# An S5 stage with its y stores on other queues: burst outputs count as done one slot sooner, half of the stores of y on ScalarE, y's load and GELU issued sooner

## The chip, the core and the metric

The kernel runs on one core of a Trainium2 chip. It is timed in microseconds of device time, as the median of several runs. The core has engines that each run their own instructions in order: TensorE (PE, matrix products; its weight loads are shown apart as PEld), VectorE (DVE), ScalarE (ACT), GpSimd (POOL) and SyncE (SP). DMAs are begun by an instruction on one of the engines, mostly SP and POOL here, and then run beside them.

## What is computed

One step of a two-layer decoder trunk for 256 new prompt tokens and 8 sample tokens, 264 columns in all, in float32. The first layer is a short gated convolution, the second an S5 state-space mixer with a GLU. What matters here is the S5 mixer:

```python
proj = h @ w_in                       # 2048 -> 2 * 4096
u, z = jnp.split(proj, 2, axis=-1)
bu = einsum('tbgh,gph->tbgp', u, b_bar)
bu[0] += lam_bar * carry
states = associative_scan(a2*a1, a2*b1 + b2)      # over tokens, complex
y = real(einsum('ghp,tbgp->tbgh', c_c, states))
y = gelu(y + d_skip * u)
y = y * sigmoid(y @ w_glu + b_glu)                # 4096 -> 4096
out = (y * silu(z)) @ w_out                       # 4096 -> 2048
return out, real(h_last), imag(h_last)
```

There are 256 groups of 16 channels and 64 complex states.

## The kernel before

**Slots.** All weight products are cut into 640 slots, one for a block of 1024 x 128 weights: 24 matmuls of 264 columns, three for each of eight 128 x 128 blocks, since a float32 product is made of three products of split operands (wh times H, wh times L, wl times H). `load_raw` brings 1 MB of raw weights for two slots on SP (L187), `conv_h` makes wh on ACT (L196), `conv_l` makes wl on DVE (L205). Buffers: three of raw, four of wh, three of wl. Slots 320 to 383 make u, 384 to 447 make z, 448 to 575 the GLU (the first 18 of them, 448 to 465, need y tiles 0 to 23; slot 466 and on needs y tiles 24 to 31), 576 to 639 the output.

**The order.** `Stream.go` writes the program out slot by slot: per slot the raw load six slots ahead, then the running procedures (generators), then wh three slots ahead, wl two ahead, the matmuls, and side work such as the scan. A procedure that yields a number goes on that many slots later; one that yields `Lag(us)` goes on when the plan's own clock `run.t` is that much later. What is written out first comes first on its engine, and each engine and each DMA queue works in that order.

**The S5 stage** lies beside slots 340 to 466. The 256 groups are handled in four quarters (q):

- `v_proc` multiplies u by the chunk operator vt on PE in half-bursts of 16 matmuls (L893), eight per quarter, each into both ps_a buffers; ACT evacuates them into S (L907). From q = 2 on they wait for `tw_done`, since the S of two quarters before is overwritten.
- `scan_proc` runs 63 steps per quarter on DVE (L931 to L936), with parts of wl between them.
- `state_out` transposes the last states, ACT copies them to so and sp (L975, L976), and SP stores them with six DMAs (L979, L981). sp shares its buffers (tag "ut") with ut of `u_out` (L852) and with zt.
- `tw_proc` makes y for eight channel blocks at a time: 16 bursts in all, burst i of 64 matmuls on PE (L1017, L1021) into both ps_b buffers. `tw_done` is set to i + 1 two slots later. It releases the loads of uct, yt and tt for burst i + 2 (`tw_load`, on POOL) and the v half-bursts two quarters on.
- `tw_evac` copies the burst to yo on ACT (L1031), one slot later stores yo to y_d in DRAM with ten DMAs (L1039, L1042), five per jj, begun by POOL for jj = 0 and by SP for jj = 1; `Lag(Y_ST)` later SP loads it back as yb in the layout of the GLU (L1045), and `Lag(Y_LD)` after that ACT makes the GELU (L1047). `split4` then splits each y tile for PE (L258 on ACT, L259 on DVE).

The DMAs that SP and ACT begin take eight semaphores in turn, in the order of the program (DMAHW0 to DMAHW7 in the listings below, those of POOL have DMASW0 to DMASW7). Where the listing names a DMAHW semaphore on a store, the instruction waits for the DMA that used that semaphore last.

Of the kernel before, what the change touches and what calls it, by code (L numbers as in the profile page):

```python
# [40 lines left out]
class Stream:  # L41
# [11 lines left out]
    def spawn(self, gen, wait):  # L53
        self.procs.append([self.now + wait, 0.0, gen])
# [70 lines left out]
def tile_hybrid_conv_s5_step(  # L125
# [7 lines left out]
    PE, V, A, P = nc.tensor, nc.vector, nc.scalar, nc.gpsimd  # L133
    mult, add, sub = ALU.mult, ALU.add, ALU.subtract
    wq, mq = nc.sync, nc.sync
# [678 lines left out]
    def ssm_stage():  # L814
        conv_ctx.close()
        ss["ybp"] = ctx.enter_context(tc.tile_pool(name="ybp", bufs=1))
        ss["yb"] = ss["ybp"].tile([128, KI, T], F32, name="yb32")
        ss["sw"] = sw = ctx.enter_context(tc.tile_pool(name="sw", bufs=2))
        ss["S1"] = sw.tile([128, NSL // 2, GB, 2], F32, name="S1", bufs=1)
        ss["uct"] = [sw.tile([128, 8, TC], F32, name=f"uct{p}", bufs=1) for p in range(2)]  # L820
        ss["sv_p"] = tc.tile_pool(name="sv", bufs=1)
        ss["sv"] = sv = ss["sv_p"].__enter__()
        ss["S0"] = sv.tile([128, NSL // 2, GB, 2], F32, name="S0")
        ss["ucv"] = [sv.tile([128, 8, CB], F32, name=f"ucv{p}") for p in range(2)]
        for p in range(2):
            P.memset(ss["ucv"][p][:, :, NCH:], 0.0)
            P.memset(ss["uct"][p][:, :, 0:Z], 0.0)
            P.memset(ss["uct"][p][:, :, TC - 1:], 0.0)
        for i in range(2):
            P.memset(ss[f"S{i}"][:, NS // 2], 0.0)  # L830
        spawn(v_load(), 0)
        spawn(v_proc(), 0)
        spawn(tw_load(), 0)
        spawn(tw_proc(), 0)
        spawn(split_pool(), 0)
        side(scan_proc())

    def slot(S, i):

        return S[:, i // 2, :, i % 2]  # L840
# [116 lines left out]
    def state_out(q, S):  # L957
        while fin_done[0] <= q or bank_a[0] == run.now or bank_b[0] == run.now:
            yield 1
        sw, bank = ss["sw"], "ps_a" if q < NB - 1 else "ps_b"  # L960
        gs = slice(q * GB, (q + 1) * GB)
        so = sw.tile([128, 4, 2, SD], F32, name="so", tag="big", bufs=1)
        sp = sw.tile([GB, 2, SD], F32, name="sp", **(dict(tag="ut") if q < NB - 1 else dict(tag="uct0", bufs=1)))
        ps = pss.tile([128, 512], F32, name=bank)
        for i in range(4):
            a = (Z + 1 + NCH) // 2 + i
            PE.transpose(ps[:, i * 128:(i + 1) * 128], S[:, a].rearrange("p g b -> p (g b)"), ident)
        ps2 = pss.tile([128, 512], F32, name="ps_b")
        PE.transpose(ps2[:GB, :128], slot(S, Z + NCH), ident)
        so_done[0] = q + 1  # L970
        yield 1
        pv = ps.rearrange("p (i pb c pi) -> p i pb c pi", i=4, pb=4, c=2)
        pv2 = ps2[:, :128].rearrange("p (pb c pi) -> p pb c pi", pb=4, c=2)
        for c in range(2):
            A.activation(so[:, :, c, :].rearrange("p i (pb pi) -> p i pb pi", pb=4), pv[:, :, :, c, :], AF.Copy)  # L975
            A.activation(sp[:, c, :].rearrange("p (pb pi) -> p pb pi", pb=4), pv2[:GB, :, c, :], AF.Copy)  # L976
        yield 1
        for c, (dp, ds_) in enumerate(((nre_prompt, nre_sample), (nim_prompt, nim_sample))):
            mq.dma_start(dp[0, 0, gs, :], sp[:, c, :])  # L979
            for b2 in range(2):  # L980
                mq.dma_start(ds_[0, b2::2, gs, :].rearrange("i g p -> g i p"), so[b2::2, :, c, :])  # L981
# [13 lines left out]
    def tw_proc():  # L995
        sw = ss["sw"]
        for q in range(NB):
            S = ss[f"S{q % 2}"]
            while scan_done[0] <= q:
                yield 1  # L1000
            if q < NB - 1:
                spawn(state_out(q, S), 0)
            for i in range(q * TB // 2, (q + 1) * TB // 2):
                while i not in tl or run.t < tl[i][2]:
                    yield 1
                yt, tt, _ = tl.pop(i)
                uc = ss["uct"][i % 2]
                yo = sw.tile([128, 8, TC], F32, name="yo")
                g0 = (2 * i - q * TB) * 8
                ps = [pss.tile([128, 512], F32, name="ps_b") for _ in range(2)]  # L1010
                bank_b[0] = run.now
                out = lambda k, g, jj: ps[g][jj * 64:jj * 64 + 64, k * TC:(k + 1) * TC]
                for k in range(4):
                    for g in range(2):
                        for jj in range(2):
                            r = slice(g * 64, g * 64 + 64)
                            PE.matmul(out(k, g, jj), tt[r, jj, k, :], uc[r, jj * 4 + k, :], start=k == 0, stop=False)  # L1017
                for k in range(4):
                    for g in range(2):
                        for jj in range(2):  # L1020
                            PE.matmul(out(k, g, jj), yt[:, jj, 2 * k + g].rearrange("p s h -> p (s h)"),  # L1021
                                      S[:, 0:TC // 2, g0 + jj * 8 + 2 * k + g, :], start=False, stop=k == 3)
                run.extra += 2.0
                for g in range(2):
                    spawn(tw_evac(i, yo, g, ps[g]), 1)
                yield 2
                tw_done[0] = i + 1
        spawn(state_out(NB - 1, S), 2)

    def tw_evac(i, yo, p, ps):  # L1030
        A.activation(yo.rearrange("p (k g) c -> p k g c", g=2)[:, :, p], ps[:, :4 * TC].rearrange("p (k c) -> p k c", c=TC), AF.Copy)  # L1031
        if p == 0:
            return
        yield 1
        for jj in range(2):
            rows = y_d[2 * i + jj].rearrange("(x h) t -> h x t", h=GS)
            a = jj * 64
            dq = P if 5 * jj < Y_POOL else mq
            dq.dma_start(rows[:, :, NP:], yo[a:a + GS, :, 0:NS])  # L1039
            for s in range(LC):  # L1040
                dq = P if 5 * jj + s + 1 < Y_POOL else mq
                dq.dma_start(rows[:, :, s * NCH:(s + 1) * NCH], yo[a + s * GS:a + (s + 1) * GS, :, Z:Z + NCH])  # L1042
        yield Lag(Y_ST)
        yv = ss["yb"][:, 2 * i:2 * i + 2, :]
        lq.dma_start(yv, y_d[2 * i:2 * i + 2].rearrange("j p t -> p j t"))  # L1045
        yield Lag(Y_LD)
        A.activation(yv, yv, AF.Gelu_apprx_tanh)  # L1047
        y_done[0] = 2 * i + 2
# [127 lines left out]


    n_ssm, n_glu = n_conv_in + 64, n_conv_in + 64 + 128
    U_LAG, Y_ST, Y_LD, T_BUFS = 8.0, 11.0, 10.0, 2
    V_BUFS, Y_POOL, U_ST = 2, 5, 6.0  # L1180
    C_T, C_S, zq, lq, sq = 0.3, 0.2, P, mq, P
    B_CONV, B_OUT, B_U, B_Z = 1.1, 1.3, 1.35, 1.65
    ctx.enter_context(tc.manual_schedule())
# [74 lines left out]
```

## Time and profile before

| | us |
|---|---|
| median of 3 runs | 2071.18 |
| lowest and highest | 2069.71, 2071.76 |
| the profiled execution | 2072.58 |
| its span in the trace | 2070.8 |
| PE busy in it | 2026.1 (98%) |
| DVE busy | 1486.8 (72%) |
| ACT busy | 946.1 (46%) |
| POOL busy | 184.1 (9%) |

The span is what the trace shows between the first and the last instruction; the profiled execution's own time lies 1.8 us above it. PE is busy nearly all of the time, so the few windows in which it isn't are to be looked for, and what ends its waits there. The 16 bursts of y lie at 1207 to 1525 us of the span, the GLU starts at about 1450, with its fourth part waiting for the last y tiles at 1525 to 1540.

### The profile page before, as it was taken

The page shows a single profiled execution, that of the slowest core. Times are in us where ns is not written, and L with a number is a line of the kernel's source. Part 1 is how long each engine was busy: PE and PEld are TensorE (multiplying, and loading weights), DVE is VectorE, ACT ScalarE, POOL GpSimd, SP SyncE. Part 2 cuts the span into 40 slices and gives each one's busy share as a digit, 9 for nine tenths or more (in the row PEclk, how much of TensorE's full clock was granted, in tenths as well). Part 3 has the DMA queues.
Part 4 walks back from the last instruction along what each step waited for, and adds up shares of the span by engine and source line. Part 5 has one row for each costly group of instructions (what it writes and reads, how often), then busy time and mean ns, then how long its engine had stood idle before and what let it go on. Part 6 is the DMA issues. An engine that isn't in the chain of part 4 may idle for free. (4 is left out here: it accounts for less than half of the span.)

```text
span 2070.8 us, 44488 instructions
## 1 busy us (share of the span) xinstructions
PE 2026.1 (98%) x17796; PEld 1996.5 (96%) x17796; DVE 1486.8 (72%) x3818; ACT 946.1 (46%) x1417; POOL 184.1 (9%) x341
## 2 busy tenths in 40 slices
PE   8999999999999999999999999999889999999997
PEld 7999999999999999999999999999789999999997
DVE  6784557999999999555548989999935555566443
ACT  6447554444444444444434334444444444455443
POOL 0000000000000000000143243514120000000000
PEclk9999999999999999999999999999999999999998
DMA  7656776677677677766687779879576566555653
GB/s 230 212 184 208 241 232 198 204 237 216 204 229 216 208 225 219 220 206 203 195 278 236 221 230 289 266 244 292 162 209 194 181 194 197 191 184 187 194 179 108
DMA packets 446707, 441.35 MB, mean 213 GB/s; under 512 B 69914, under 2 KB 428300, under 8 KB 445964
## 3 DMA queue, kind: packets, MB, share of 16 engines
q1 hardware_dynamic: 430340, 398.05, 62.4%
q0 software_dynamic: 16128, 40.45, 6.2%
q8 instruction: 139, 2.28, 0.4%
q14 instruction: 68, 0.56, 0.1%
q10 hardware_dynamic: 32, 0.01, 0.0%
HBM read 391.42 MB, written 47.15 MB: 212 GB/s over the span
## 5 line engine op out<-in xcount | busy, mean ns | idle before, releaser
L230 PE MATMUL acc_ps<-s,wh 128*128 128x264 f32 x4544 | 1308.8, 288 | 9.2 <-ACT s L258 7.4
L233 PE MATMUL acc_ps<-s,wl 128*128 128x264 f32 x4528 | 1288.3, 285 | 4.8 <-DVE wl L205 4.8
L196 ACT ACTIVATE wh<-raw 128x1024 fp32r<-128x1024 f32 x640 | 677.8, 1060 | 909.7 <-PE acc_ps L231 698.3
L205 DVE TENSOR_TENSOR wl<-raw,wh 128x1024 fp32r<-128x1024 f32 (+2 forms) x960 | 826.2, 865 | 365.6 <-PE acc_ps L233 228.0
L230 PEld LDWEIGHTS acc_ps<-s,wh 128*128 128x128 f32 x4544 | 859.5, 189 | 16.0 <-ACT s L258 8.2
L231 PE MATMUL acc_ps<-s,wh 128*128 128x264 f32 x3072 | 872.9, 284 | 0.0
L233 PEld LDWEIGHTS acc_ps<-s,wl 128*128 128x128 f32 x4528 | 852.4, 188 | 7.1 <-DVE wl L205 7.1
L231 PEld LDWEIGHTS acc_ps<-s,wh 128*128 128x128 f32 x3072 | 581.5, 189 | 0.0
L231 PE MATMUL acc_ps<-l,wh 128*128 128x264 f32 x1472 | 420.5, 286 | 2.3 <-DVE l L259 2.2
L231 PEld LDWEIGHTS acc_ps<-l,wh 128*128 128x128 f32 x1472 | 278.2, 189 | 3.3 <-DVE l L259 3.3
L932 DVE STREAM_SHUFFLE S<-S 128x64 f32<-128x64 f32 x252 | 74.9, 297 | 0.0
L230 PE MATMUL acc_ps<-yb,wh 128*128 128x264 f32 x256 | 72.9, 285 | 0.0
L230 PE MATMUL acc_ps<-ya,wh 128*128 128x264 f32 x256 | 72.8, 284 | 0.0
L231 PE MATMUL acc_ps<-yb,wh 128*128 128x264 f32 x256 | 72.7, 284 | 0.0
L233 PE MATMUL acc_ps<-ya,wl 128*128 128x264 f32 x256 | 72.6, 284 | 0.0
L233 PE MATMUL acc_ps<-yb,wl 128*128 128x264 f32 x256 | 72.5, 283 | 0.0
L231 PE MATMUL acc_ps<-ya,wh 128*128 128x264 f32 x256 | 72.5, 283 | 0.0
L714 POOL MEMSET ue<- 128x2 f32 x32 | 3.8, 123 | 624.1 <-DVE cv L726 564.9
L936 DVE TENSOR_TENSOR S<-S,prod 128x64 f32<-128x64 f32 x252 | 55.9, 222 | 2.3
L931 DVE TENSOR_TENSOR prod<-S,lam 128x64 f32<-128x64 f32 x252 | 55.5, 220 | 1.9
L934 DVE TENSOR_TENSOR prod<-S,lam 128x64 f32<-128x64 f32 x252 | 56.9, 226 | 0.0
L933 DVE TENSOR_TENSOR S<-S,prod 128x64 f32<-128x64 f32 x252 | 56.4, 224 | 0.0
(317 smaller groups left out, 1763.9 us busy)
## 6 DMA issues: line engine op xcount, KB each, us to landing
raw<-in_conv_w_in_dram SPq DMA_DIRECT2D x127, 1024.0 KB, 6.1
raw<-in_ssm_w_in_dram SPq DMA_DIRECT2D x64, 1024.0 KB, 6.8
raw<-in_ssm_w_glu_dram SPq DMA_DIRECT2D x64, 1024.0 KB, 5.1
raw<-in_conv_w_out_dram SPq DMA_DIRECT2D x32, 1024.0 KB, 5.5
raw<-in_ssm_w_out_dram SPq DMA_DIRECT2D x32, 1024.0 KB, 5.1
yt_d<-Y SPq DMA_DIRECT2D x32, 256.0 KB, 7.2
vt_d<-vt SPq DMA_DIRECT2D x32, 256.0 KB, 7.0
vt<-vt_d POOLq DMA_DIRECT2D x16, 512.0 KB, 7.8
```

The lines of the kernel that those rows point to most:

```text
L196: A.activation(whs[i], raws[i][:, :, m * 128:(m + 1) * 128], AF.Copy)
L205: run.fill(lambda k=k: V.tensor_tensor(wls[i][:, k], raws[i][:, k, m * 128:(m + 1) * 128], whs[i][:, k], op=sub))
L230: PE.matmul(ps, wh[:, k, :], H(kt), start=first, stop=False)
L231: PE.matmul(ps, wh[:, k, :], L(kt), start=False, stop=False)
L233: PE.matmul(ps, wl[:, k, :], H(kt), start=False, stop=last)
L714: P.memset(halves(0)[:, :, 0:1], 0.0)
L931: V.tensor_tensor(pr[:, 0], cur, a4[:, 0], op=mult)
L932: V.stream_shuffle(sh, cur, SWAP)
L933: V.tensor_tensor(nxt, nxt, pr[:, 0], op=add)
L934: V.tensor_tensor(pr[:, 1], sh, a4[:, 1], op=mult)
L936: V.tensor_tensor(nxt, nxt, pr[:, 1], op=add)
```

## The change

`tw_done` is set one slot after the burst, not two (the evacuations still come one slot after it). The stores of jj = 0 are begun by ACT, in order with its conversions and evacuations; those of jj = 1 by POOL; SP begins none any more. `Y_ST` and `Y_LD`, the lags before yb's load and before the GELU, go from 11 and 10 to 9 and 8.

```diff
@@ -1023,8 +1023,9 @@
                 run.extra += 2.0
                 for g in range(2):
                     spawn(tw_evac(i, yo, g, ps[g]), 1)
-                yield 2
+                yield 1
                 tw_done[0] = i + 1
+                yield 1
         spawn(state_out(NB - 1, S), 2)
 
     def tw_evac(i, yo, p, ps):
@@ -1035,10 +1036,9 @@
         for jj in range(2):
             rows = y_d[2 * i + jj].rearrange("(x h) t -> h x t", h=GS)
             a = jj * 64
-            dq = P if 5 * jj < Y_POOL else mq
+            dq = P if jj else A
             dq.dma_start(rows[:, :, NP:], yo[a:a + GS, :, 0:NS])
             for s in range(LC):
-                dq = P if 5 * jj + s + 1 < Y_POOL else mq
                 dq.dma_start(rows[:, :, s * NCH:(s + 1) * NCH], yo[a + s * GS:a + (s + 1) * GS, :, Z:Z + NCH])
         yield Lag(Y_ST)
         yv = ss["yb"][:, 2 * i:2 * i + 2, :]
@@ -1176,8 +1176,8 @@
 
 
     n_ssm, n_glu = n_conv_in + 64, n_conv_in + 64 + 128
-    U_LAG, Y_ST, Y_LD, T_BUFS = 8.0, 11.0, 10.0, 2
-    V_BUFS, Y_POOL, U_ST = 2, 5, 6.0
+    U_LAG, Y_ST, Y_LD, T_BUFS = 8.0, 9.0, 8.0, 2
+    V_BUFS, U_ST = 2, 6.0
     C_T, C_S, zq, lq, sq = 0.3, 0.2, P, mq, P
     B_CONV, B_OUT, B_U, B_Z = 1.1, 1.3, 1.35, 1.65
     ctx.enter_context(tc.manual_schedule())
```

In the changed kernel the lines after the first piece are one higher: the evacuation is L1032, the stores are L1040 and L1042.

**ACT around burst 2** (slots 381 to 386), before. L975 and L976 are the copies of the state, L196 makes wh, L1031 evacuates a burst, L907 evacuates a half-burst of v:

```order
L976 ACTIVATE sp<-ps_b 64x64
L196 ACTIVATE wh<-raw 128x1024 [waits PE_49,Activation_49]
L1031 ACTIVATE yo<-ps_b 128x4x74 [waits PE_49] x2
L196 ACTIVATE wh<-raw 128x1024 [waits DVE_49,DMAHW0_49,PE_49,Activation_49]
L907 ACTIVATE S_12647<-ps_a 128x4x36x2 [waits PE_49] x2
L196 ACTIVATE wh<-raw 128x1024 [waits DVE_49,PE_49,Activation_49]
L907 ACTIVATE S_12647<-ps_a 128x4x36x2 [waits PE_49] x2
L196 ACTIVATE wh<-raw 128x1024 [waits DVE_49,DMAHW1_49,PE_49,Activation_49]
```

and after:

```order
L976 ACTIVATE sp<-ps_b 64x64
L1040 DMA y_d<-yo 16x8x8 [waits Activation_49]
L1042 DMA y_d<-yo 16x8x64 x3
L1042 DMA y_d<-yo 16x8x64 [waits DMAHW1_49]
L196 ACTIVATE wh<-raw 128x1024 [waits PE_49]
L907 ACTIVATE S_12647<-ps_a 128x4x36x2 [waits PE_49] x2
L1032 ACTIVATE yo<-ps_b 128x4x74 [waits PE_49] x2
L196 ACTIVATE wh<-raw 128x1024 [waits DMAHW0_49,DVE_49,PE_49]
L1040 DMA y_d<-yo 16x8x8 [waits DMAHW5_49,Activation_49]
L1042 DMA y_d<-yo 16x8x64 [waits DMAHW6_49]
L1042 DMA y_d<-yo 16x8x64 [waits DMAHW0_49]
L907 ACTIVATE S_12647<-ps_a 128x4x36x2 [waits PE_49] x2
```

The first burst's five stores now come behind the state copies (the first of them right behind), the next burst's five stand between its evacuation and the second evacuation of a v half-burst, and a v half-burst (L907) comes ahead of burst 2's evacuation.

**SP at the state stores** of the first cluster, before. L1039 and L1042 are stores of y, L979 stores sp, L981 stores so:

```order
L187 DMA raw<-in_ssm_w_in_dram 128x8x256 [waits DMAHW6_49,DVE_49,Activation_49]
L1039 DMA y_d<-yo 16x8x8 [waits Activation_49]
L1042 DMA y_d<-yo 16x8x64 x4
L979 DMA out_dram<-sp 64x64 [waits DMAHW7_49,Activation_49]
L981 DMA out_dram<-so 64x4x64 [waits DMAHW0_49]
L981 DMA out_dram<-so 64x4x64 [waits DMAHW1_49]
L979 DMA out_dram<-sp 64x64 [waits DMAHW2_49,Activation_49]
L981 DMA out_dram<-so 64x4x64 [waits DMAHW3_49]
```

and after:

```order
L187 DMA raw<-in_ssm_w_in_dram 128x8x256 [waits DMAHW6_49,DVE_49,Activation_49]
L979 DMA out_dram<-sp 64x64 [waits Activation_49]
L981 DMA out_dram<-so 64x4x64 [waits DMAHW7_49]
L981 DMA out_dram<-so 64x4x64 [waits DMAHW0_49]
L979 DMA out_dram<-sp 64x64 [waits DMAHW2_49,Activation_49]
L981 DMA out_dram<-so 64x4x64 [waits DMAHW3_49]
L981 DMA out_dram<-so 64x4x64 [waits DMAHW4_49]
```

The five stores of y ahead of the state stores are gone, and the semaphores that the state stores wait for have other last users: the second L979 waits for DMAHW2, which ACT's second store of burst 1 used last; the so store behind it waits for DMAHW3, used last by the raw in the first row here.

**ACT at the end of the stage** (bursts 15 and 16), before. L1047 is the table load and the GELU, L258 the split:

```order
L196 ACTIVATE wh<-raw 128x1024 [waits DMAHW4_49,DVE_49,PE_49]
L1031 ACTIVATE yo<-ps_b 128x4x74 [waits DMAHW0_49,DMASW7_49,DMAHW1_49,DMASW6_49,DMAHW5_49,DMASW5_49,DMAHW6_49,DMASW1_49,DMAHW7_49,DMASW0_49,PE_49]
L1031 ACTIVATE yo<-ps_b 128x4x74 [waits PE_49]
L1047 ACT_TABLE_LOAD
L1047 ACTIVATE yb_12637<-yb_12637 128x528 [waits DMAHW3_49]
L258 ACTIVATE s_99<-yb_12637 128x264 [waits Activation_49]
L1047 ACTIVATE yb_12637<-yb_12637 128x528 [waits DMAHW5_49]
L258 ACTIVATE s_99<-yb_12637 128x264 [waits Activation_49]
L975 ACTIVATE so<-ps_b 128x4x64 [waits PE_49]
L976 ACTIVATE sp<-ps_b 64x64 [waits DMASW2_49,PE_49,Pool_49]
L1047 ACTIVATE yb_12637<-yb_12637 128x528 [waits DMAHW0_49]
```

and after:

```order
L258 ACTIVATE s_99<-yb_12637 128x264
L1032 ACTIVATE yo<-ps_b 128x4x74 [waits DMASW4_49,DMASW3_49,DMASW5_49,DMASW2_49,DMAHW6_49,DMASW1_49,PE_49]
L1032 ACTIVATE yo<-ps_b 128x4x74 [waits PE_49]
L196 ACTIVATE wh<-raw 128x1024 [waits DVE_49,PE_49]
L1040 DMA y_d<-yo 16x8x8 [waits DMAHW4_49,Activation_49]
L1042 DMA y_d<-yo 16x8x64 [waits DMAHW5_49]
L1042 DMA y_d<-yo 16x8x64 [waits DMAHW6_49]
L1047 ACTIVATE yb_12637<-yb_12637 128x528
L258 ACTIVATE s_99<-yb_12637 128x264 [waits Activation_49]
L975 ACTIVATE so<-ps_b 128x4x64 [waits PE_49]
L976 ACTIVATE sp<-ps_b 64x64 [waits PE_49,Pool_49]
L1047 ACTIVATE yb_12637<-yb_12637 128x528 [waits DMAHW3_49]
```

The last evacuation comes behind the first of these GELUs and its splits instead of ahead of it; behind that evacuation stand a wh and burst 16's five stores, then the second GELU, and the state copies after it. On PE burst 15 is written in front of slot 463 instead of 464, and burst 16 in front of 465 instead of 466; in the earlier quarters bursts 2, 3 and 4 follow each other by two slots (380, 382, 384, 386; before 380, 382, 386, 388).

## Rows read from the trace of the kernel before

**Rows 1.** By stages: window, its length, busy PE, PEld, DVE, ACT, POOL; clock, DMA.
```profile
1250.00:1300.00 50.00, 49.41 (x422) 48.36 (x421) 49.59 (x285) 22.12 (x34) 13.30 (x21) 1.00 0.87 275
1300.00:1350.00 50.00, 48.75 (x627) 46.15 (x626) 48.93 (x266) 23.24 (x44) 26.53 (x43) 1.00 0.91 275
...
1450.00:1500.00 50.00, 42.08 (x372) 39.58 (x371) 48.64 (x187) 23.49 (x42) 5.14 (x9) 1.00 0.50 162
1500.00:1550.00 50.00, 42.14 (x455) 39.83 (x454) 17.65 (x22) 23.15 (x37) 12.37 (x23) 0.90 0.70 204
```

**Rows 2.** Timeline of DVE, then PE: start, length, what, [idle before, its releaser].
```profile
1232.39 0.43 DVE L852 TENSOR_TENSOR ut<-acc_ps,Rn 128x264 f32<-128x264 f32 x1 [7.89 <-DMA out_dram<-sp]
...
1493.74 1.26 PE L1021 MATMUL ps_b<-S,yt 128*64 128x74 f32 x32 [1.95 <-DVE S L936]
```

**Rows 3.** Timeline of SP, 1215 to 1228.
```profile
1215.62 0.57 SPq L1039 DMA_DIRECT2D y_d<-yo  x1
1216.24 3.65 SPq L1042 DMA_DIRECT2D y_d<-yo  x4
1219.99 0.54 SPq L979 DMA_DIRECT2D out_dram<-sp  x1
1220.57 6.65 SPq L981 DMA_DIRECT2D out_dram<-so  x2
1227.32 0.56 SPq L979 DMA_DIRECT2D out_dram<-sp  x1
```

**Rows 4.** Waits of the SP queue, 1195 to 1240: total, times, longest.
```profile
SPq L981 <- DMA raw<-in_ssm_w_in_dram: 5.3, 1, 5.3
```

**Rows 5.** Timeline of the tail: ACT, SP and PE.
```profile
1529.16 0.36 ACT L975 ACTIVATE so<-ps_b 128x256 f32<-128x256 f32 x1
1529.65 0.51 SPq L979 DMA_DIRECT2D out_dram<-sp  x1
...
1533.67 0.41 SPq L1045 DMA_DIRECT2D yb<-y_d  x1
1536.59 0.64 ACT L1047 ACTIVATE yb<-yb 128x528 f32<-128x528 f32 x1 [3.73 <-DMA yb<-y_d]
...
1537.74 0.59 PE L230 MATMUL acc_ps<-s,wh 128*128 128x264 f32 x1 [3.79 <-ACT s L258]
```

**Rows 6.** Landings: y_d of POOL (1210), sp (1227), so (1227), so (1322).
```profile
DMA to landing us min/median/max: 4.2/4.5/5.0
...
DMA to landing us min/median/max: 4.8/4.8/4.8
...
DMA to landing us min/median/max: 3.4/3.4/3.4
...
DMA to landing us min/median/max: 4.8/5.1/5.3
```

**Rows 7.** Timeline of PE and DVE around 1415.
```profile
1414.14 0.75 PE L1017 MATMUL ps_b<-uct,tt 64*64 64x74 f32 x32
...
1416.34 0.42 DVE L205 TENSOR_TENSOR wl<-raw,wh 128x256 fp32r<-128x256 f32 x1
```

**Rows 8.** Timeline of PE and ACT around the bursts.
```profile
1215.27 0.75 PE L1017 MATMUL ps_b<-uct,tt 64*64 64x74 f32 x32
...
1220.24 1.11 PE L893 MATMUL ps_a<-ucv,vt 64*128 64x72 f32 x16
...
1224.40 1.12 PE L893 MATMUL ps_a<-ucv,vt 64*128 64x72 f32 x16
...
1225.54 0.74 ACT L907 ACTIVATE S<-ps_a 128x288 f32<-128x288 f32 x2
...
1312.19 0.75 PE L1017 MATMUL ps_b<-uct,tt 64*64 64x74 f32 x32
```

**Rows 9.** Landing of the raw begun at 1215.20, then of that at 1315.34.
```profile
DMA to landing us min/median/max: 11.4/11.4/11.4
...
DMA to landing us min/median/max: 6.6/6.6/6.6
```

## The prediction, made before the changed kernel had run

> **What bounds the kernel now.** I read the table by stages first. Outside the S5 stage TensorE (PE) is busy all the time; there the only idle windows are those of [rows 1]: 0.59 us in 1250 to 1300, 1.25 in 1300 to 1350, 7.92 in 1450 to 1500 and 7.86 in 1500 to 1550. In the first three VectorE (DVE) is busy 49.59, 48.93 and 48.64 of 50: from 1232 to near 1495 the scan and the wl conversions on DVE are the bound, and PE waits for DVE, last 1.95 us at 1493.74 for the scan's last step [rows 2]. In the fourth both wait: PE stands in front of the GELU of the last y tiles, and its granted clock is 0.90 (between the full 2.4 GHz level and the 1.2 GHz one).
>
> The timeline of DVE comes second. Just before its long stretch DVE has one hole: 7.89 us, ended by the landing of a store of sp [rows 2]. It stands in front of a ut whose buffer is shared with sp. The timeline of SyncE (SP) shows why the landing is so late [rows 3]: four y stores take 3.65 us, the first sp store leaves at 1219.99, and the second of the two so stores behind it holds SP until 1227.32, so the second sp store leaves only then. The waits of SP name the reason [rows 4]: 5.3 us for the landing of a weight load, raw. The so store needs nothing from raw; but the order of SP shows eight DMAHW semaphores handed out in turn to all DMAs of SP and ScalarE (ACT), and a DMA waits until the last user of its semaphore has landed. That rule decides this forecast. It holds in the row for SP; the change brings such waits to ACT: five y stores for each of 16 bursts, with ACT's own conversions and evacuations in order behind them.
>
> Last I read the tail, 1524 to 1540 [rows 5]: state copies at 1529.16 behind two GELUs, SP's six state stores from 1529.65, the last yb load behind them at 1533.67, the last GELU at 1536.59 (3.73 of it waited for that load), PE's last piece at 1537.74 (3.79 waited).
>
> **The DVE hole: gain of up to 4.0.** SP loses its y stores. The second sp store then waits for ACT's second y store of the first burst. ACT begins these after the copies of so and sp, at about 1214; with the landing of such a store, 4.2 to 5.0 [rows 6], it is in by about 1219 to 1219.5. The second sp store leaves then and lands 4.8 later, as in [rows 6], about 1224: where it was 1232, so the hole of 7.89 goes nearly whole. It cannot all be kept. DVE may run ahead of PE only as far as the three wl buffers reach: at 1416.34 DVE starts to write a wl into the buffer that PE had finished with when it began the burst of 1414.14 [rows 7], so the slack is 2.2 us. PE can move up only by its own idle time, 0.59 + 1.25 = 1.84. Cap: 2.2 + 1.84 = 4.0.
>
> **First cluster (bursts 1 to 4): a stall of 1.1 to 5.9.** Bursts come a slot closer, and a half-burst of v now stands ahead of burst 2. A half-burst with its slot takes 1224.40 − 1220.24 = 4.16, and itself 1.11 [rows 8]. PE would reach the third v half-burst at 1215.27 + 1.11 + 1.95 (burst) + 2.93 (slot) + 4.16 = 1225.4. It needs the evacuation of the second one, 0.74 on ACT [rows 8], and that is queued behind burst 2's five stores. The last of these waits for an so store of SP, which itself waits for the raw of 1215.20. As the trace has it, raw lands after 11.4, at 1226.6 [rows 9]; the so store lands 3.4 later [rows 6], at 1230.0; with 0.5 of issue (SP's 0.54 in [rows 3]) and the evacuation PE goes on at 1231.3: a stall of 5.9. With the 6.6 that another raw took [rows 9] it is 1.1. Nothing on the trace shows how raw lands once the y stores leave from another engine, since the bytes are the same; I take the middle, 3.5, and keep both ends.
>
> **Second cluster (bursts 5 to 8): PE 6.4 late, net 4.2.** The pattern returns. PE reaches the third half-burst at 1312.19 + 1.11 + 1.95 + 2.93 + 4.16 = 1322.3 [rows 8]. Here the second sp store waits for the raw of 1315.34, which landed after 6.6, at 1321.9 [rows 9]; it lands 4.8 later and the so stores behind it 4.8 to 5.3 [rows 6], at about 1327.5; with issue and evacuation ACT is done at 1328.7. PE is 6.4 late against before, whatever it had lost in the first cluster, as long as that raw leaves when it did. DVE, which has 2.2 of slack, is then 6.4 − 2.2 = 4.2 late, and from there to 1495 it is the bound and gets nothing back: **+4.2**. The DVE gain is spent here. If DVE comes to this place 4.0 ahead, raw leaves 4.0 sooner and +0.2 is left. If it comes late by the slow first cluster (5.9 − 2.2 = 3.7), raw leaves that much later: +7.9.
>
> **Third cluster and the rest: 0, at most 3.** No v bursts follow bursts 9 to 12, so no evacuation stands behind the stores but those of y; wh conversions do. ACT would be blocked for about as long as in the second cluster, 1320 to 1328, and wh is made three slots ahead, 8.8. The earlier yb loads and GELUs (Y_ST, Y_LD) cost nothing and give nothing for bursts 1 to 12: they are due long before PE asks for those tiles at 1524. POOL's loads for burst i+2 now go ahead of its y stores; nobody waited for them on the path, so 0.
>
> **Tail: +0.8.** Burst 16 moves one slot ahead, −2.93. But the state copies now have burst 16's five stores (5 × 0.54 = 2.70) and one more wh (1.06) ahead of them on ACT: −2.93 + 2.70 + 1.06 = +0.83. The six state stores follow the copies and the last yb load follows these, so the last GELU moves with them. If ACT's issue is hidden, −1.9; if burst 15's five stores come onto the path too, +3.5. ACT's stores have no row of their own; SP's and POOL's price stands for them.
>
> The Trainium skill speaks for the change here: "DMA: Bandwidth & Descriptors", section "Issuing engines are not separate DMA queues", says that DMAs begun by several engines share the same 16 DMA engines and interleave, and that using more engines only saves a sequencer's issue time. By that alone SP would be 4.2 us sooner at the state stores and ACT would lose as much where it has time, which is the first rival below. The 5.3 us in [rows 4] are a wait at issue that this sentence doesn't cover.
>
> **Sum.** Against the profiled execution (2072.58, span 2070.8): +4.2 + 0.8 = +5.0, 2077.6. That execution lies 1.4 over the median of the timed runs, and I carry the difference over: 2071.18 + 5.0 = **2076.2**. Its own range, from the ends of the second cluster's middle part (+2) and of the tail, is 2073 to 2080. A measurement of this kernel can tell about 0.2%, 4.1 us, from no change.
>
> **Rivals.**
> *Faster: the hole goes and ACT is free in time.* Place: ACT at the evacuation of the second half-burst. Price: −4.0 from DVE, tail between −1.9 and +0.8: 2065.3 to 2068.0, say 2067. For it: 7.89 us is the largest single hole, and the store that caused it does leave SP's queue earlier. Against: the wait for raw only changes engines. It decides if ACT is through burst 2's stores by 1224.6, which takes a landing of raw under 1224.6 − 0.5 − 3.4 − 1215.2 = 5.5, and through burst 6's by 1321.6, which needs that raw to leave over 6 us sooner. Chance 0.17.
> *Same: gain and stall cancel.* DVE comes to the second cluster 4.0 ahead, PE still waits there: +0.2, with the tail 2072.2. Also here: the change does not do what it says where it counts, since the last GELU stays behind the six state stores. Needs the fast end of the first cluster, a raw that lands like the 6.6. Chance 0.23.
> *Much slower: the first cluster at its slow end,* +7.9 + 0.8: 2079.9, and with the tail's upper end 2082.6. Needs the raw of 1215 to land as it did. Chance 0.20.
> *Forecast,* 2076: chance 0.40, of which a quarter ends within 0.2%.
>
> Faster: 0.16 of the first rival. Same: 0.23 + 0.10 + 0.01 = 0.34. Slower: 0.30 + 0.20 = 0.50. The range, 2066.5 to 2082.5, leaves out the better half of the first rival and a few per cent above.
>
> **What would show it.** Right: the wait of DVE's ut near 1224 falls under 2 us; ACT shows waits of several us at L1042 stores that end with landings of SP's DMAs; PE shows new idle time at L893 near 1225 and 1322, ended by ACT; DVE's scan ends 3 to 8 us later; the last GELU within 2 us of where it was against the end of the scan. Wrong: no idle PE at L893 (then the first rival), or stores on ACT that hold it for less than their issue; a tail whose state stores leave 2 us sooner; or DVE waiting for wh in the third cluster, which I put at nothing.

## The result: slower by 16 us, three times what was forecast

The changed kernel takes 2087.55 us (median of 4 runs, 2084.47 to 2089.68), the kernel before 2071.47 (4 runs): a ratio of 1.0074, with a 95% interval of 1.0058 to 1.0090. The forecast was 2076.2, its range ended at 2082.5. The direction was right and so was the stage, the size was not.

| profiled execution | before | after |
|---|---|---|
| its own time | 2072.58 | 2085.79 |
| span | 2070.8 | 2084.0 |
| first of the 252 scan steps on DVE (its L936) | 1099.00 | 1100.82 |
| 246th of them | 1482.96 | 1496.55 |

Of the 13.2 us between the spans, 1.8 were there before the S5 stage was reached, where the two programs are the same; the profiled executions of the kernels below begin the scan between 1094.96 and 1101.14. So times of the stage are compared from its first scan step on, which takes 1.82 off every time of the changed kernel: the scan's end, read at the 246th step, comes (1496.55 − 1482.96) − 1.82 = 11.8 us late.

The stages of the changed kernel, against [rows 1] (window, its length, busy PE, PEld, DVE, ACT, POOL; clock, DMA share, GB/s):

```profile
1200.00:1250.00 50.00, 46.97 (x584) 44.69 (x583) 42.88 (x225) 19.77 (x34) 30.01 (x48) 0.93 0.88 265
1250.00:1300.00 50.00, 48.39 (x416) 47.66 (x416) 45.89 (x260) 21.95 (x34) 9.99 (x16) 1.00 0.78 244
1300.00:1350.00 50.00, 47.33 (x599) 45.31 (x597) 44.51 (x241) 20.17 (x39) 24.94 (x40) 0.97 0.86 254
1350.00:1400.00 50.00, 49.21 (x424) 48.41 (x423) 47.47 (x268) 22.23 (x35) 9.33 (x17) 1.00 0.73 228
```

From 1200 to 1400 PE is idle 3.03 + 1.61 + 2.67 + 0.79 = 8.1 us, where it was idle 1.84, and its granted clock, 1.00 in all of these windows before, is 0.93 and 0.97 in two of them. What PE waits for, and what ACT waits for, over the whole stage (the lists of waits: total, times, longest):

```profile
PE ps_a L893 <- ACT S L907: 8.1, 4, 3.0
```

```profile
ACT S L907 <- DMA y_d<-yo: 15.7, 5, 5.6
...
ACT wh L196 <- DMA y_d<-yo: 14.2, 3, 6.6
...
ACT zt L861 <- DMA y_d<-yo: 11.8, 2, 8.3
```

None of these rows exists in the trace of before. ACT stands 41.7 us where the profile names a y store as what ended the wait, and four times PE stands behind ACT at a half-burst of v. ACT waited before as well (18.0 us in front of wh for loads of raw, in 7 times), but then PE never stood behind it at L893: what counts is what is queued behind the wait.

The hole of DVE [rows 2] went as forecast, and what it gave was lost at the next wait. DVE's rows:

```profile
1227.37 0.43 DVE L852 TENSOR_TENSOR ut<-acc_ps,Rn 128x264 f32<-128x264 f32 x1 [0.88 <-DMA y_d<-yo]
...
1239.74 0.42 DVE L205 TENSOR_TENSOR wl<-raw,wh 128x256 fp32r<-128x256 f32 x1 [4.50 <-PE acc_ps L233]
```

SP's rows that answer to [rows 3], and the wait that answers to [rows 4] (still there, 2.8 us):

```profile
1217.43 0.59 SPq L979 DMA_DIRECT2D out_dram<-sp  x1
1218.07 1.78 SPq L981 DMA_DIRECT2D out_dram<-so  x2
1221.11 0.51 SPq L979 DMA_DIRECT2D out_dram<-sp  x1
1224.47 1.27 SPq L981 DMA_DIRECT2D out_dram<-so  x2
```

```profile
SPq L981 <- DMA raw<-in_ssm_w_in_dram: 2.8, 1, 2.8
```

### The profile page after: what moved, and what is told of

The parts are those of the page before. It is cut to its first block, busy times and chain, and to the rows that moved or that the text cites. A ratio compares the mean times of both kernels' runs of the same rounds, so it can differ in the third digit from the quotient of the medians.

```text
span 2084.0 us, 44469 instructions
## 1 busy us (share of the span) xinstructions
PE 2034.0 (98%) x17796; PEld 2004.4 (96%) x17796; DVE 1488.6 (71%) x3818; ACT 944.9 (45%) x1417; POOL 184.6 (9%) x341
## 5 line engine op out<-in xcount | busy, mean ns | idle before, releaser
L196 ACT ACTIVATE wh<-raw 128x1024 fp32r<-128x1024 f32 x640 | 678.0, 1060 | 906.4 <-PE acc_ps L231 700.3
L936 DVE TENSOR_TENSOR S<-S,prod 128x64 f32<-128x64 f32 x252 | 55.9, 222 | 2.3
```

Source lines behind the costliest of these rows:

```text
L196: A.activation(whs[i], raws[i][:, :, m * 128:(m + 1) * 128], AF.Copy)
L936: V.tensor_tensor(nxt, nxt, pr[:, 1], op=add)
```

## The mechanism in the trace

**First cluster.** ACT around burst 2's stores, and PE behind it:

```profile
1223.23 1.08 ACT L196 ACTIVATE wh<-raw 128x1024 fp32r<-128x1024 f32 x1
1223.39 0.31 ACTq L1040 DMA_DIRECT2D y_d<-yo  x1
1224.63 5.21 ACTq L1042 DMA_DIRECT2D y_d<-yo  x4
1229.89 0.72 ACT L907 ACTIVATE S<-ps_a 128x288 f32<-128x288 f32 x2 [5.58 <-DMA y_d<-yo]
```

```profile
1230.36 2.29 PE L893 MATMUL ps_a<-ucv,vt 64*128 64x72 f32 x16 [3.03 <-ACT S L907]
```

Burst 2's last store waits for the semaphore of the so store that SP began at 1224.47, and that one had itself waited for a raw (2.8 us, the row above). The four stores take 5.21 us, though the issue of one is 0.31 in the row above them; the evacuation comes 5.58 late, and PE waits 3.03. The half-burst then takes 2.29 instead of the 1.11 of [rows 8]. The clock shows why (windows of 5 us):

```profile
1225.00:1230.00 5.00, 2.33 (x20) 2.12 (x18) 4.12 (x24) 0.11 (x1) 3.51 (x7) 1.00 0.93 256
1230.00:1235.00 5.00, 4.64 (x68) 4.36 (x70) 4.72 (x31) 2.29 (x5) 3.13 (x5) 0.53 1.03 348
1235.00:1240.00 5.00, 5.00 (x50) 4.71 (x47) 0.50 (x3) 1.18 (x3) 4.35 (x9) 0.79 0.78 245
...
1325.00:1330.00 5.00, 2.33 (x22) 2.04 (x21) 3.32 (x19) 3.50 (x7) 3.04 (x5) 0.93 0.56 143
1330.00:1335.00 5.00, 5.00 (x43) 4.79 (x42) 2.42 (x15) 1.78 (x3) 3.96 (x7) 0.73 0.94 247
```

After the idle time the granted clock is 0.53 in 1230 to 1235, near the 1.2 GHz level (in the single microseconds from 1231 to 1237 it is 0.50), then 0.79, and full again from 1240. What is missing to full clock is (0.47 + 0.21) × 5 = 3.4 us here and (0.07 + 0.27) × 5 = 1.7 at the second place: 5.1 us in all, on top of the 8.1 of idle time.

PE's next wait, 1.61 in front of 1254.52, has another cause: burst 4's last store has, by the program's listing, the semaphore of the yb load that SP began at 1242.79, and that load landed 10.9 us later, at 1253.7. The evacuation follows at 1254.05.

**Second cluster.** Here ACT stood at burst 5's stores (1317.38 to 1322.72) and then at zt. zt's buffer comes free when a z store lands; POOL had begun that store at 1320.18, behind its own y stores, and it landed 6.0 later, at 1326.2 (the profile names the y store, which had ended before). The evacuation came behind zt:

```profile
1319.00 3.72 ACTq L1042 DMA_DIRECT2D y_d<-yo  x2
1326.27 0.39 ACT L861 ACTIVATE zt<-acc_ps 128x264 f32<-128x264 f32 x1 [8.29 <-DMA y_d<-yo]
...
1327.51 0.71 ACT L907 ACTIVATE S<-ps_a 128x288 f32<-128x288 f32 x2
```

```profile
1319.66 0.53 POOL L1042 DMA_DIRECT2D y_d<-yo  x1 [2.77 <-DMA uct<-us_d]
1320.18 0.58 POOL L863 DMA_DIRECT2D z_d<-zt  x1
```

```profile
1327.97 1.41 PE L893 MATMUL ps_a<-ucv,vt 64*128 64x72 f32 x16 [2.67 <-ACT S L907]
```

So ACT's own stores did not set the 2.67 of this place: they were through 3.5 us before zt could begin. POOL was late: it stood 2.77 at its last y store, for a load of uct that took 7.5 us to land, and began the z store 7.5 after the start of burst 5's evacuation (1320.18 − 1312.64). In e1 below, with the same bursts and no store on ACT, that load landed in 4.0, the z store left 4.75 after the evacuation's start (1304.60 − 1299.85), and PE waited 0.25 behind the same zt:

```profile
1304.60 0.58 POOL L863 DMA_DIRECT2D z_d<-zt  x1
...
1311.08 0.39 ACT L861 ACTIVATE zt<-acc_ps 128x264 f32<-128x264 f32 x1 [5.87 <-DMA z_d<-zt]
...
1312.77 1.42 PE L893 MATMUL ps_a<-ucv,vt 64*128 64x72 f32 x16 [0.25 <-ACT S L907]
```

Why the load landed later in the changed kernel was not followed.

**The sum that the trace gives.** PE's idle time 8.1, plus the clock's 5.1, less the 1.84 of idle time that PE had before: 11.4 us late. Read directly it is a little less: burst 9, which stands in front of slot 430 in both kernels, begins 10.7 late (1404.55 − 1392.05 − 1.82); the 0.7 between was not followed. DVE is 9.9 late at the 169th scan step (1374.60 − 1362.89 − 1.82) and 10.0 at the 185th (1397.10 − 1385.25 − 1.82), so it had 0.7 of slack. In the third cluster one wl waited 1.47 us for a wh behind the stores; DVE is 11.6 late after it and 11.8 at the end.

## The experiments

Each was compared with the kernel before on the same chip. The kernels:

| kernel | us | before | ratio (95% interval) |
|---|---|---|---|
| e1, the change, old queues | 2067.68 | 2069.61 | 0.9990 (0.9977 to 1.0004) |
| e2, new queues alone | 2100.06 | 2069.61 | 1.0146 (1.0128 to 1.0164) |
| e3, the change, all stores on POOL | 2102.43 | 2069.61 | 1.0154 (1.0136 to 1.0171) |
| e6, before, all stores on POOL | 2104.81 | 2069.61 | 1.0174 (1.0157 to 1.0190) |
| e8, new queues for bursts 1 to 8 | 2082.07 | 2070.84 | 1.0054 (1.0037 to 1.0071) |
| e9, new queues for bursts 9 to 16 | 2071.85 | 2070.84 | 1.0001 (0.9992 to 1.0009) |
| e4, the change, state stores on POOL | 2079.41 | 2070.84 | 1.0045 (1.0030 to 1.0061) |
| e7, e1 and own buffer for sp | 2066.70 | 2070.84 | 0.9984 (0.9975 to 0.9993) |
| e5, before, own buffer for sp | 2070.11 | 2072.83 | 0.9989 (0.9974 to 1.0003) |
| e10, the change, z stores on SP | 2096.13 | 2072.83 | 1.0114 (1.0096 to 1.0133) |
| e12, before, the lags alone | 2073.08 | 2072.83 | 1.0005 (0.9991 to 1.0019) |
| e14, e7 and last state stores on POOL | 2062.98 | 2072.83 | 0.9956 (0.9939 to 0.9972) |

The theory: ACT stands at its stores until the last users of their semaphores have landed, and what is queued behind it (evacuations, wh) holds PE and DVE. The rivals: the closer bursts crowd PE; the issue of 80 DMAs costs ACT its time; POOL's new order does it, which is what the rows of the second cluster above point at for their place.

### Queues or bursts: e1 and e2

e1 is the change without its queues:

```diff
-                yield 2
+                yield 1
                 tw_done[0] = i + 1
+                yield 1
...
-    U_LAG, Y_ST, Y_LD, T_BUFS = 8.0, 11.0, 10.0, 2
+    U_LAG, Y_ST, Y_LD, T_BUFS = 8.0, 9.0, 8.0, 2
```

> The change without its queues: tw_done one slot after the burst and the lags 9 and 8, but y stores begun by POOL and SP as before. Theory (ACT stands at its y stores, waiting for the landing of the DMA that used their semaphore last, and the evacuations behind it hold PE): no store is on ACT, so no L907 waits for a y_d landing, PE has no idle time at L893, and the time is 2068 to 2074, within 0.2% of before. Rival (the bursts that follow each other by two slots and the half-burst of v ahead of burst 2 crowd PE and ACT): PE waits at L893 all the same, 2080 to 2088.

Measured: 2067.68 against 2069.61, no difference that its interval shows. PE has 0.25 us of idle time from 1200 to 1450 and full clock. Its scan ends 3.45 us earlier (1476.81 − 1482.96 + 2.70).

e2 is the new queues alone:

```diff
-            dq = P if 5 * jj < Y_POOL else mq
+            dq = P if jj else A
             dq.dma_start(rows[:, :, NP:], yo[a:a + GS, :, 0:NS])
             for s in range(LC):
-                dq = P if 5 * jj + s + 1 < Y_POOL else mq
```

> The queues alone: the stores of jj = 0 on ACT and of jj = 1 on POOL, with tw_done two slots after the burst and the lags 11 and 10 as before. Theory (waits of ACT at its stores): most of the 16 us is here, 2079 to 2090; ACT waits 25 to 45 us in all for y_d landings, PE 4 to 9 us at L893, with the granted clock at about half in the 5 to 10 us after each of PE's longer waits. Rival (crowded bursts): 2068 to 2074.

Measured: 2100.06, 30 us slower. That is above the range that I had written down, and nearly twice the changed kernel's loss. The waits of PE, and the longest of ACT's:

```profile
PE ps_a L893 <- ACT S L907: 13.3, 3, 7.1
```

```profile
1331.55 0.35 ACTq L1039 DMA_DIRECT2D y_d<-yo  x1
1331.94 4.12 ACTq L1041 DMA_DIRECT2D y_d<-yo  x4
1336.11 0.71 ACT L907 ACTIVATE S<-ps_a 128x288 f32<-128x288 f32 x2 [9.86 <-DMA y_d<-yo]
```

With the old spacing burst 6's stores stand ahead of the first evacuation of a v half-burst, not between the first and the second one, and its first store alone waited from 1326.25 to 1331.55. SP had the same wait there: its second sp store left at 1330.77, when the raw begun at 1320.6 had landed (10.1 us). So the queues are the loss. The closer bursts soften it; that one half-burst of v is then ahead of the stores fits this place (7.1 us of PE's time here, 2.67 in the changed kernel), but no run takes it alone. The rival of the crowded bursts falls with both runs.

### Where it is lost: e8 and e9

Both are the changed kernel, with the new queues for one half of the bursts and the old ones for the other; e9 has `>=` for `<`:

```diff
-            dq = P if jj else A
+            on_act = i < NC2 // 2
+            dq = (P if jj else A) if on_act else (mq if jj else P)
```

> The changed kernel with its new queues for bursts 1 to 8 alone; bursts 9 to 16 store as before (jj = 0 on POOL, jj = 1 on SP). Theory (stores on ACT hold the evacuations of v half-bursts, which exist only beside bursts 1 to 8): nearly all of the loss stays, 2080 to 2086; idle PE at L893 as in the changed kernel, 6 to 9 us. Rival (the loss comes from wh behind the stores, or from the tail): 2070 to 2076.

> The mirror image: bursts 1 to 8 store as before, bursts 9 to 16 with the new queues. Theory: no v half-burst comes after burst 8, so only wh is late in the third cluster (DVE waited 1.5 us for it in the changed kernel) and the tail moves by under 2 us: 2068 to 2073, 1 to 4 us over the 2067.7 of the change with the old queues. Rival (wh and tail): 2078 and over.

Measured: e8 2082.07 (+11.2 of the changed kernel's 16.1), e9 2071.85 (+1.0, no difference). PE waits 11.3 us for evacuations at L893 in e8 and 0.3 in e9, though in e9 ACT still stood behind its stores:

```profile
PE ps_a L893 <- ACT S L907: 11.3, 4, 3.6
```

```profile
ACT wh L196 <- DMA y_d<-yo: 8.4, 2, 6.0
...
PE ps_a L893 <- ACT S L907: 0.3, 1, 0.3
```

Most of the loss lies where the v half-bursts are, which exist beside bursts 1 to 8 alone. wh is converted early enough to hide most of a wait of 6.0 (DVE waited 1.6 for one). That e9 equals the kernel before does not make its queues free: e1, which has its bursts and lags, ends the scan 3.45 earlier than before, e9 only 1.46, so the new queues cost 2.0 there.

### The wait or the issue: e4

```diff
-            mq.dma_start(dp[0, 0, gs, :], sp[:, c, :])
+            P.dma_start(dp[0, 0, gs, :], sp[:, c, :])
...
-                mq.dma_start(ds_[0, b2::2, gs, :].rearrange("i g p -> g i p"), so[b2::2, :, c, :])
+                P.dma_start(ds_[0, b2::2, gs, :].rearrange("i g p -> g i p"), so[b2::2, :, c, :])
```

> The changed kernel with the six state stores of each quarter begun by POOL instead of SP, so that five issues per burst stay on ACT, but the DMAs whose semaphores they take over are mostly ACT's own earlier stores. Theory (ACT stands at the semaphores, above all behind the state stores of SP): ACT's waits for y_d landings fall to under half of the 42 us of the changed kernel, 2072 to 2082. Rival (the issue of DMAs on ACT itself costs): unchanged or slower, 2085 to 2092. POOL, with six more issues per cluster, can give some of it back.

Measured: 2079.41, 8.6 slower than before on its chip, where the changed kernel lost 16.1. ACT begins the same 80 stores, but the waits at them fall from 41.7 us to 6.2 + 4.5 + 3.9 = 14.6 (the last of these ends with a yb load that used the semaphore before):

```profile
ACT zt L861 <- DMA z_d<-zt: 16.5, 3, 9.8
...
ACT S L907 <- DMA y_d<-yo: 6.2, 2, 4.6
ACT wh L196 <- DMA y_d<-yo: 4.5, 2, 2.7
ACT S L907 <- DMA yb<-y_d: 3.9, 2, 2.0
```

So about half of the loss (16.1 to 8.6, on two chips) went with the waits at the state stores, while all 80 issues stayed on ACT. PE's four waits have become two:

```profile
PE ps_a L893 <- ACT S L907: 6.5, 2, 4.2
```

One, 2.33 in front of 1249.28, is behind burst 4's stores, the last of which has the semaphore of a yb load here too. The other, 4.21 in front of 1325.81, is behind zt: POOL, with six more issues per cluster, begins the z stores late (the upper row). What is left has waits of its own, so these runs don't show what the issue of the stores costs by itself.

### POOL instead of ACT: e3 and e6

e3 is the changed kernel with `dq = P` for all ten stores, e6 the kernel before with `Y_POOL = 10`.

> The changed kernel with all ten stores of a burst on POOL, none on ACT or SP. Theory (waits of ACT): no wait of ACT for a y_d landing, no idle PE at L893; SP begins the second sp store soon after the first, so DVE's ut no longer waits 7.9 us near 1224, and 0 to 4 us are gained: 2066 to 2072. Rival (crowded bursts): 2080 and over. Rival (POOL's ten issues of 0.53, 5.3 us of every 7.8 between bursts, delay its loads of uct, yt, tt and u): idle PE at L1017 or L893 that ends with a load's landing, 2074 to 2082.

> The kernel before with all ten stores of a burst on POOL. Theory: SP is free, the second sp store leaves early, DVE's wait of 7.9 us in front of ut goes; DVE can keep only what PE's idle time (1.8 us) and the slack of the wl buffers allow: 2066 to 2071, 0 to 5 us under before. If DVE's hole cost nothing: 2070 to 2072. If POOL is too full: 2073 to 2080.

Measured: 2102.43 and 2104.81. Both expectations of the theory were wrong, and both times are far beyond what the rival of a full POOL was given (2074 to 2082 and 2073 to 2080). POOL has its own semaphores in turn and is in order too; with ten stores per burst it begins its loads and z stores too late. ACT's wait for z stores, and one of PE's for a load, in e3:

```profile
ACT zt L861 <- DMA z_d<-zt: 33.3, 6, 10.4
```

```profile
1443.97 1.26 PE L1017 MATMUL ps_b<-uct,tt 64*64 64x74 f32 x32 [6.12 <-DMA tt<-tt_d]
```

The hole of DVE was gone in e3 and e6 as in the changed kernel; it did not help. Of the three queues SP was the one with room for the five stores.

### Is zt's wait a cause of its own: e10

```diff
-    C_T, C_S, zq, lq, sq = 0.3, 0.2, P, mq, P
+    C_T, C_S, zq, lq, sq = 0.3, 0.2, mq, mq, P
```

> The changed kernel with the stores of z begun by SP instead of POOL. In its second cluster ACT stood 8.3 us at zt, whose buffer is free when a z store lands that POOL began behind its y stores; the evacuation of a v half-burst came behind. If that wait is a cause of its own: it goes, idle PE near 1328 falls from 2.7 us to under 1, 2076 to 2084. If ACT's own stores set the time there: 2084 to 2090. SP then also waits at z stores ahead of its raw loads, and the semaphores of z come into the turn of ACT's stores, which can make it slower than the changed kernel, over 2090.

Measured: 2096.13. With the z stores on SP they join the turn of ACT's semaphores; zt waits more (23.4 us in 4 times) and PE waits 12.8 at L893. So it tells only that SP is no place for them. The trace of e4 tells more: there burst 5's stores are through at 1315.91, ACT stands 9.83 at zt, until 1324.11, for a z store that POOL began at 1316.69, and PE waits 4.21 for the evacuation behind it. zt's wait can stop PE with no wait at a y store in front of it.

### The hole, the lags, and a faster kernel: e5, e12, e7, e14

e5 gives sp its own buffer in the kernel before, e7 in e1:

```diff
-        sp = sw.tile([GB, 2, SD], F32, name="sp", **(dict(tag="ut") if q < NB - 1 else dict(tag="uct0", bufs=1)))
+        sp = sw.tile([GB, 2, SD], F32, name="sp", **(dict(tag="sp", bufs=1) if q < NB - 1 else dict(tag="uct0", bufs=1)))
```

> The kernel before with sp in a buffer of its own, nothing else: the price of DVE's hole of 7.9 us near 1224. Theory (the step on the hole in the prediction: DVE can keep only what PE's idle time, 1.8, and the slack of the wl buffers, 2.2, allow): the hole goes, the scan ends 3 to 5 us earlier, 2066 to 2069. If the hole was worth all of it: 7 us less, 2063. If PE set the stage anyway: no difference.

> The change with the old queues (2067.7 us on its first chip) and sp in a buffer of its own, so that ut no longer waits for the landing of an sp store. Theory (DVE keeps a lead only as far as PE's idle time and the wl buffers allow, 4.0): DVE's wait of 3.3 us near 1225 goes, the lead goes up from 4.6 by at most 1, and the time falls by 0 to 2 us against that kernel, 2064 to 2068. If DVE alone set the stage: 3 us less. If nothing waited for that hole: the same.

Measured: e5 2070.11 against 2072.83, no difference that its interval shows, and above the 2066 to 2069 expected; in the profile DVE is 7.5 us ahead at the 78th step and 3.5 at the 246th, and the span keeps 1.3 of it. e7 2066.70 against 2070.84: 0.9984, an interval that ends below 1; 7.7 ahead at the 78th step and 4.0 at the 246th. In both PE has no idle time left from 1200 to 1450 (the row is e7's):

```profile
1200.00:1450.00 250.00, 250.00 (x2731) 243.44 (x2730) 242.99 (x1317) 116.33 (x196) 102.02 (x166) 1.00 0.88 270
```

At the scan's end the hole is worth 3.5 to 4.0 of its 7.9 us, as the prediction's cap said: after that PE is the bound.

e12 is the second piece of e1's diff alone.

> The kernel before with the lags 9 and 8 alone (yb's load and the GELU written one slot or two earlier). Theory: these are due long before PE asks for the tiles, and in the tail the last yb load stays behind the six state stores: within 2 us of before, 2069 to 2073. Rival (the GELU is what the 2 us of the change with the old queues came from): 2066 to 2068.

Measured: 2073.08 against 2072.83, no difference. It was not free inside the stage, though: the scan ends 3.0 us late and PE is idle 4.25 from 1200 to 1450. The cause is the theory's own, with another instruction: the earlier GELU stands on ACT 6.90 and 8.29 us for a yb load, an evacuation of a burst is queued behind it, and PE waits 1.90 and 2.35 for that. The tail gave none of it back (without the offset the span is 3.5 longer); this execution had reached the stage 2.9 us earlier than before, and the interval of the runs, which reaches to 1.0019 or 3.9 us, can't tell 3 us from none.

e14 is e7 with the last quarter's state stores on POOL:

```diff
+            oq = mq if q < NB - 1 else P
-            mq.dma_start(dp[0, 0, gs, :], sp[:, c, :])
+            oq.dma_start(dp[0, 0, gs, :], sp[:, c, :])
...
-                mq.dma_start(ds_[0, b2::2, gs, :].rearrange("i g p -> g i p"), so[b2::2, :, c, :])
+                oq.dma_start(ds_[0, b2::2, gs, :].rearrange("i g p -> g i p"), so[b2::2, :, c, :])
```

> The change with the old queues, sp in its own buffer (2066.7 us on its chip), and the last quarter's six state stores on POOL, which is idle by then, so that the last yb load doesn't queue behind them on SP. Theory: the last yb load leaves 2 to 4 us sooner, unless the landing of the last y stores (about 3 us) then holds it; PE's last wait for a GELU falls from 2.9 us to 0.5 to 2: 2063 to 2066, under both kernels. Rival (y stores' landing takes over the whole wait): 2066 to 2067.

Measured: 2062.98 against 2072.83, a ratio of 0.9956 (0.9939 to 0.9972): faster than both kernels. SP begins the last two yb loads one behind the other, and PE's last wait for a GELU is 1.01 us, where it was 3.79 [rows 5]:

```profile
1517.49 1.86 SPq L1044 DMA_DIRECT2D y_d<-yo  x4
1519.59 3.31 SPq L1047 DMA_DIRECT2D yb<-y_d  x2
```

```profile
1526.55 0.59 PE L230 MATMUL acc_ps<-s,wh 128*128 128x264 f32 x1 [1.01 <-ACT s L258]
```

## Why the prediction was wrong, step by step

- **DVE's hole.** Right: 7.89 us became 0.88, and DVE was 7.7 us ahead at the 78th step. The cap of 4.0 is what e5 and e7 kept at the end (3.5 and 4.0). Its two parts were not right, and that they make 4.0 together is luck: in e7 PE's burst 9 begins 3.3 earlier (1386.18 − 1392.05 + 2.60), not 1.84, and DVE has 0.7 of slack beyond that, not 2.2.
- **First cluster, stall of 1.1 to 5.9, middle 3.5.** Right: 3.03, at the third half-burst and by the chain of semaphores that was named. But it was the only stall in the sum; burst 4's stores made another of 1.61 at 1254.52, by the landing of a yb load, which the prediction did not look at.
- **The clock.** This term was missing. After two of PE's waits the granted clock fell, to 0.53 in the worst 5 us, and 5.1 us went with it. The prediction had read a clock under 1 only in the tail.
- **Second cluster, "PE is 6.4 late against before, whatever it had lost in the first cluster".** This step failed. It let the second cluster's wait absorb what PE had lost, since that wait was to end with a raw that leaves at its old time. The wait that came was another one: burst 5's stores and zt, not burst 6's stores. All that it hangs on (the stores of ACT and POOL, the z store behind POOL's) begins after PE has made burst 5, and burst 5, in front of slot 406 in both kernels, came 6.7 late (1310.78 − 1302.26 − 1.82). At burst 9 PE is 10.7 late. So the second cluster added 4.0 to the first one's 6.7 and absorbed nothing. The raw did not keep its time either: it left at 1319.62, with the offset taken off 2.5 late, as DVE was; but it did not set this wait.
- **Slack of 2.2.** It was 0.7 (10.7 − 10.0).
- **Third cluster, 0 and at most 3.** 1.5 in the profile of the changed kernel; in e9, with the new queues from there on, 2.0 against e1.
- **Tail, +0.8.** It gave 0.4 back (11.4 between the spans without the offset, 11.8 at the scan's end). The term −2.93 was too large: the evacuation of burst 16 comes only 0.9 earlier against the scan's end, (1537.15 − 1524.50) − 13.59, since a GELU and its splits stand ahead of it now. In turn these no longer stand between it and the state copies, which the sum had left out, and ACT's five stores took 2.25 (1538.34 to 1540.59), not 2.70: from the evacuation to the copies it is 4.81 (1541.96 − 1537.15), where it was 4.66. The last GELU comes 0.5 earlier, though it waits longer. The rows that answer to [rows 5]:

```profile
1537.15 0.71 ACT L1032 ACTIVATE yo<-ps_b 128x296 f32<-128x296 f32 x2
...
1541.96 0.36 ACT L975 ACTIVATE so<-ps_b 128x256 f32<-128x256 f32 x1
1542.45 0.51 SPq L979 DMA_DIRECT2D out_dram<-sp  x1
...
1546.82 0.40 SPq L1045 DMA_DIRECT2D yb<-y_d  x1
1549.66 0.64 ACT L1047 ACTIVATE yb<-yb 128x528 f32<-128x528 f32 x1 [5.56 <-DMA yb<-y_d]
...
1550.81 0.59 PE L230 MATMUL acc_ps<-s,wh 128*128 128x264 f32 x1 [5.03 <-ACT s L258]
```

So of the forecast's +5.0 the S5 stage was to give 4.2 and gave 11.8. In the first cluster the mechanism and its place were right. What failed is the second cluster (a wait with another cause, and stalls of the first cluster taken as absorbed by it, where 4.0 came on top of 6.7) and a term that was left out (the clock, 5.1). The forecast's 4.2 rested on the wait named for the second cluster; that wait did not stop PE (ACT stood 1.41 at burst 6's stores there), so that the direction came out right is luck in this part. Of the 16 us between the medians the profile explains the 13.2 between the profiled executions, less the 1.8 ahead of the stage; the other timed executions were up to 4 us longer than the profiled one, and what was longer in them is open. How much the changed kernel's POOL, whose z store stopped ACT in the second cluster, owes to the new queues is open too.

The Trainium skill's sentence on issuing engines ("DMA: Bandwidth & Descriptors", section "Issuing engines are not separate DMA queues"), that several of them only save issue time, describes a gain that was not what decided here: in e2 the same stores on other issuing engines cost 30 us, by the waits of the issuing engine.

## What to carry to other kernels

A DMA begun by a compute engine puts its waits into that engine's order: look up in the program's listing which semaphore each one waits for, and what stands behind it, before moving it. Where semaphores are handed out in turn to several queues, a store can wait for a weight load that it has nothing to do with. Ask the same of every instruction that can wait on such an engine: here a GELU in front of its load and a copy in front of a store's landing stopped PE just as the stores did. A wait of PE can cost more than its length, so look at the granted clock in the rows behind it. And before one stall is let to cover the next, ask whether what ends the second one begins after the first.

## What the runs showed that was not expected

Five stores in a row that wait for nothing long take 2.25 us on ACT, 0.45 each, and 0.53 each on POOL (2.10 for four). The length of PE's wait alone doesn't tell what its clock does: over the 5 us behind it the granted clock was 0.50 after 3.03 us (1230.36), 0.66 after 2.67 (1327.97) and 1.00 after 1.61 (1254.52) in the changed kernel; behind the 1.95 in front of the scan's last step it was 1.00 in the kernel before (1493.74) and 0.66 in e1 (1487.64). And POOL, busy 100.94 of the 250 us from 1200 to 1450 before, had no room for five more stores per burst: moving them there cost 33 (e3) and 35 us (e6).
